# A second MLP with chunk 0 plain and chunks 1 and 2 by Strassen's seven products

## Chip, core and metric

One core of one Trainium2 chip runs the program alone. The metric is device microseconds from the first to the last instruction and what lies around them, as the median of several executions. TensorE (PE) multiplies, VectorE (DVE) and ScalarE (ACT) do elementwise work, GpSimd (POOL) a little of it, and SyncE (SP) issues nearly all DMAs. Each engine takes its own list of instructions in order.

## What is computed

A two-layer backbone on 1152 tokens (1024 latent, 128 context) of width 1024: attention and an MLP, then a bidirectional state-space layer with a gated unit (glu) and a second MLP, then a final norm. The MLP, on the modulated norm h of x, is

```python
def _mlp(h, w1, w2):
    a = jax.nn.relu(h @ w1)
    return (a * a) @ w2
...
xx = xx + g2x * _mlp(_modulate(xx, norm2_g[i], sh2x, sc2x), mlp_w1[i], mlp_w2[i])
...
y_sample = _rmsnorm(xx, final_norm_g)
```

with w1 of 1024 x 4096, w2 of 4096 x 1024, all in float32.

## The kernel before

Tokens lie in three chunks of 384 columns (`NCH`, `CW`), channels in eight tiles of 128 partitions (`KT`); chunk 2 ends with the context tokens, which have another modulation, so its elementwise operations come in pieces of 256 and 128 (`pieces`). A float32 product is made of three matmuls of a faster type: each operand is split into a high part (a cast on ACT, L51) and a low part (source minus high on DVE, L52), and `mm3` (L45 to L47) issues high x high, high x low, low x high.

```python
        mm(out, lh, rh, start=first, stop=False)
        mm(out, lh, rl, start=False, stop=False)
        mm(out, ll, rh, start=False, stop=last)
```

`mlp(layer)` walks over 16 blocks of 256 hidden units. A block loads its w1 and w2 (each in two raw tiles of 512 KB, L658, from a pair of buffers `wr`, and split into one high and one low tile). For each chunk the first product makes two tiles of 128 hidden units from eight tiles of h (48 matmuls); relu, square and split follow (L683, L684, L51, L52). Then for each chunk the second product makes eight tiles of 128 channels from the two (48 matmuls), and `add_x` (L455) adds each, times its gate, to x. A block is 288 matmuls of 128x384. At the start of the second MLP the h of chunk 0 is there already (from `glu`); those of chunks 1 and 2 are made by `norm_apply` (L234, L237, L238), chunk 2's after its `norm_stats`. The last block runs the final norm's statistics, and `final(c)` writes chunks 0 and 1 with ACT and POOL (L1241, L1242) beside the next chunk's products, and chunk 2 at the end with DVE (L1244).

Engine lists are ordered by the framework's scheduler from priorities in program order and its own estimate of when operands are ready; tile pools with a fixed number of buffers per tag decide which instruction waits for which.

Of the kernel before, what the change touches and what calls it, by code (L numbers as in the profile page):

```python
# [20 lines left out]
KT = 8  # L21
NCH = 3
CW = 384
HD = 64
DFF = 4096
# [8 lines left out]
class Body:  # L34
# [600 lines left out]
    def mlp(self, layer, bg=None):  # L635
        nc, tc, a = self.nc, self.tc, self.a
        with ExitStack() as ctx:
            M = ctx.enter_context(tc.tile_pool(name=f"mlp{layer}", bufs=1, reuse_waits="tile"))
            self.M = M
            ps = ctx.enter_context(tc.tile_pool(name=f"mlpps{layer}", bufs=6, space=PSUM))  # L640
            h = []
            for c in range(NCH):
                if c not in self.mh:
                    self.mh[c] = self.h_big(M, f"mh{c}")
                    if c == 2:
                        for _ in self.norm_stats(c):
                            pass
                    for _ in self.norm_apply(c, layer, 1, self.mh[c]):
                        pass
                h.append(self.mh[c])  # L650
            nb = DFF // 256

            def load(name, pool, tag, src):
                w = [pool.tile([128, 2048], F32R, name=name, tag=tag, bufs=2) for _ in range(2)]
                for q in range(2):
                    sl = slice(1024 * q, 1024 * q + 1024)
                    raw = self.R.tile([128, 1024], F32, name="wr", tag="wr", bufs=2)
                    nc.sync.dma_start(raw, src[:, sl])  # L658
# [5 lines left out]
            out = iter(())  # L664
            def fill(where):
                with self.tc.high_priority(offset=-self.LOW):
                    for _ in range((self.F0, self.F1)[where]):
                        next(gen, None)

            for fb in range(nb):  # L670
                w2 = load("w2", M, "w2", a["w2"][layer, fb])
                acts = []
                for c in range(NCH):
                    at = self.two_tiles(self.R, "at")
                    acts.append(at)
                    for m in range(2):
# [12 lines left out]
                for c in range(NCH):  # L689
                    stats = self.norm_stats(c, 1) if fb == nb - 1 else iter(())  # L690
                    for m in range(KT):
                        pt = ps.tile([128, 512], F32, name="m2", tag="acc")
                        for k in range(2):
                            sl = slice(1024 * k + 128 * m, 1024 * k + 128 * m + 128)
                            self.mm3(pt[:, :CW], w2[0][:, sl], w2[1][:, sl], acts[c][:, k, 0, :],
                                     acts[c][:, k, 1, :], k == 0, k == 1)
                        self.add_x(c, m, pt, layer, 1)
                        next(stats, None)
                        if m % 2:
                            next(out, None)  # L700
                    fill(1)
                    for _ in stats:
                        pass
                    if fb == nb - 1 and layer == 1:
                        out = self.final(c)
            for _ in out:
                pass
            for _ in gen:
                pass


    def cmul(self, eng, o_r, o_i, ar, ai, br, bi, t, neg=False):
# [517 lines left out]
                pass  # L1230
        self.yctx.close()

    def final(self, c):
        nc = self.nc
        for k in range(0, KT, 2):
            o = self.R.tile([128, 2, CW], F32, name="fo", tag=("wo", "wq")[k // 2 % 2] if c < 2 else "ot",
                            bufs=2 if c < 2 else 4)
            for kt in (k, k + 1):
                x, g, z = self.x[c][:, kt, :], self.gn[:, 4, kt:kt + 1], o[:, kt - k, :]
                if c < 2 or k == 6:  # L1240
# [37 lines left out]
    def run(self):  # L1278
        self.consts()
        self.start()  # L1280
        if self.stop != "s5":
            self.attention()
        if self.stop != "s5":
            if self.stop == "attn":
                return self.dump_x()
            self.mlp(0, self.background)
            if self.stop == "mlp0":
                return self.dump_x()
        else:
# [12 lines left out]

def host_consts():
# [96 lines left out]
```

## Time and profile before

| | |
|---|---|
| median of 3 runs | 2802.63 us (2799.61 to 2807.88) |
| profiled execution | 2799.74 us |
| its span, first to last instruction | 2797.8 us |
| PE busy in the span | 2609.5 us (93%) |
| DVE, ACT, POOL busy | 1824.4 us (65%), 1096.1 us (39%), 366.6 us (13%) |
| granted TensorE clock, mean | 0.979 |
| DMA | 271.67 MB, 97 GB/s |

The second MLP runs from about 1956 us to the end, with its last matmul at 2778.3 us. A matmul's record lasts about twice the distance to the next one, since two overlap; the number of records in a stretch is a few per cent short, so distances are taken from the instructions that wait for matmuls. L numbers are lines of the kernel before.

### The profile page before, as it was taken

To read this page: it belongs to the slowest core of one execution; us is meant where nothing else is said; L and a number is where in the kernel's file an instruction comes from. 1 tells how busy PE (TensorE), PEld (TensorE's weight loads), DVE (VectorE), ACT (ScalarE), POOL (GpSimd) and SP (SyncE) were. 2 spreads that over 40 slices of the span, in tenths; PEclk is the share of its full clock that TensorE was granted. 3 is DMA by queue.
4 is the path that set the end of the run, shared out by engine and by line. 5 is a ranking of instruction groups with operands and counts; after the bars stand their busy time and mean duration, and the time that the engine had idled before them with its cause. 6 is when DMAs were issued, how large, how long until landed. Compare 5 with 4: busy or idle time off the path is not lost. (4 is left out here: it accounts for less than half of the span.)

```text
span 2797.8 us, 44016 instructions
## 1 busy us (share of the span) xinstructions
PE 2609.5 (93%) x16561; PEld 2462.1 (88%) x16561; DVE 1824.4 (65%) x4342; ACT 1096.1 (39%) x2295; POOL 366.6 (13%) x476
## 2 busy tenths in 40 slices
PE   6889999998899999999899687999999999999997
PEld 4767987886699989899899676999999999999997
DVE  4847777785576787887875799545645354454455
ACT  3545666662223323332333655434422222212224
POOL 1222222210022132121220400000000000000002
PEclk8999999999999999999999799999999999999998
DMA  7353222235532233132223586433110111111101
GB/s 264 109 169 105 84 79 74 81 116 189 180 103 75 70 95 90 55 105 71 88 83 91 174 251 180 141 121 113 46 46 31 46 46 46 34 43 46 46 31 68
DMA packets 128452, 271.67 MB, mean 97 GB/s; under 512 B 13296, under 2 KB 67952, under 8 KB 126832
## 3 DMA queue, kind: packets, MB, share of 16 engines
q1 hardware_dynamic: 128240, 268.86, 30.3%
q8 instruction: 131, 2.15, 0.3%
q14 instruction: 81, 0.66, 0.1%
HBM read 214.22 MB, written 39.81 MB: 91 GB/s over the span
## 5 line engine op out<-in xcount | busy, mean ns | idle before, releaser
L455 DVE SCALAR_TENSOR_TENSOR x<-m,mod,x 128x384 f32<-128x384 f32 (+2 forms) x1024 | 496.2, 512 | 149.2 <-PE m L47 145.3
L47 PE MATMUL m<-at,w 128*128 128x384 f32 x1536 | 523.4, 341 | 0.0
L45 PE MATMUL m<-at,w 128*128 128x384 f32 x1536 | 522.7, 340 | 0.8 <-DVE x L455 0.8
L46 PE MATMUL m<-at,w 128*128 128x384 f32 x1536 | 521.7, 340 | 0.0
L45 PE MATMUL m<-mh,w 128*128 128x384 f32 x1024 | 349.1, 342 | 1.9 <-ACT mh L237 1.9
L47 PE MATMUL m<-mh,w 128*128 128x384 f32 x1024 | 349.9, 342 | 0.0
L46 PE MATMUL m<-mh,w 128*128 128x384 f32 x1024 | 349.8, 342 | 0.0
L52 DVE TENSOR_TENSOR at<-r,at 128x384 fp32r<-128x384 f32 x192 | 111.6, 583 | 361.4 <-ACT at L51 361.2
L51 ACT CAST w<-wr 128x1024 fp32r<-128x1024 f32 x128 | 131.0, 1046 | 524.4 <-PE m L46 515.7
L47 PEld LDWEIGHTS m<-at,w 128*128 128x128 f32 x1536 | 289.1, 188 | 9.2 <-issue 8.9
L45 PEld LDWEIGHTS m<-at,w 128*128 128x128 f32 x1536 | 289.2, 188 | 3.8 <-issue 1.8
L46 PEld LDWEIGHTS m<-at,w 128*128 128x128 f32 x1536 | 289.1, 188 | 2.8 <-issue 2.5
L683 ACT ACTIVATE r<-m 128x384 f32<-128x384 f32 x192 | 93.8, 490 | 373.1 <-PE m L47 370.3
L45 PEld LDWEIGHTS m<-mh,w 128*128 128x128 f32 x1024 | 193.9, 190 | 7.4 <-issue 4.8
L52 DVE TENSOR_TENSOR w<-wr,w 128x1024 fp32r<-128x1024 f32 x128 | 156.6, 1243 | 64.9 <-ACT w L51 60.6
L47 PEld LDWEIGHTS m<-mh,w 128*128 128x128 f32 x1024 | 194.5, 190 | 3.6 <-issue 3.5
L46 PEld LDWEIGHTS m<-mh,w 128*128 128x128 f32 x1024 | 194.4, 190 | 1.6 <-issue 0.8
L45 PE MATMUL m<-h,w 128*128 128x384 f32 x512 | 174.4, 341 | 1.5 <-ACT w L51 0.7
L47 PE MATMUL m<-h,w 128*128 128x384 f32 x512 | 173.9, 340 | 1.2 <-DVE w L52 1.2
L46 PE MATMUL m<-h,w 128*128 128x384 f32 x512 | 174.5, 341 | 0.0
L1242 POOL TENSOR_TENSOR fo<-fo,rb 128x384 f32<-128x384 f32 x18 | 20.6, 1176 | 1034.7 <-ACT rb L224 1026.9
L389 POOL TENSOR_SCALAR pt<-pt,sst 128x512 f32<-128x512 f32 (+1 forms) x144 | 102.6, 724 | 298.4 <-DVE sst L387 153.8
(328 smaller groups left out, 5161.1 us busy)
## 6 DMA issues: line engine op xcount, KB each, us to landing
wr<-in_w_dram SPq DMA_DIRECT2D x128, 512.0 KB, 4.4
wm<-in_w_mod_dram SPq DMA_DIRECT2D x80, 512.0 KB, 4.6
wr<-in_glu_dram SPq DMA_DIRECT2D x48, 512.0 KB, 3.3
wr<-in_w_qo_dram SPq DMA_DIRECT2D x24, 512.0 KB, 3.3
wr<-in_w_qo_dram SPq DMA_DIRECT2D x48, 256.0 KB, 2.8
bt<-bt_d SPq DMA_DIRECT2D x16, 768.0 KB, 5.5
dt_d<-d SPq DMA_DIRECT2D x32, 294.0 KB, 2.1
D<-dt_d SPq DMA_DIRECT2D x16, 588.0 KB, 4.7
```

Of the source, the lines that this page charges most:

```text
L45: mm(out, lh, rh, start=first, stop=False)
L46: mm(out, lh, rl, start=False, stop=False)
L47: mm(out, ll, rh, start=False, stop=last)
L51: (ceng.copy if ceng is self.nc.scalar else ceng.tensor_copy)(h, src)
L52: seng.tensor_tensor(out=l, in0=src, in1=h, op=ALU.subtract)
L389: nc.gpsimd.tensor_scalar(p[:, e, :nk], p[:, e, :nk], rc[:, e:e + 1], 1.0, op0=ALU.mult, op1=ALU.mult)
L455: nc.vector.scalar_tensor_tensor(out=self.x[c][:, m, lo:hi], in0=ps[:, lo:hi], scalar=self.gate(layer, j, m, s), in1=self.x[c][:, m, lo:hi ...
L683: nc.scalar.activation(r, pt[:, :CW], AF.Relu)
L1242: nc.gpsimd.tensor_tensor(out=z, in0=z, in1=self.rb[c], op=ALU.mult)
```

## The change

`run` calls a new `mlp1` in place of `mlp(1)`; the first layer's `mlp` only loses the lines that served the second. `mlp1` has two passes over the 16 blocks.

The first pass does chunk 0 alone with plain products. PE's order is: first product of block fb+1, second product of block fb. The raw loads of the next block's w1 are issued ahead of those of this block's w2. In between, `h_seven` makes the sums of chunks 1 and 2 that the products need (subtractions on POOL, each split by ACT and DVE).

The second pass does chunks 1 and 2. Their first product is a 2 x 2 block product (two halves of the inner channels, two tiles of hidden units, two chunks), done by Strassen's scheme with seven products instead of eight: `w_seven` makes seven weight parts of 128x512 from the two raw tiles of w1 (four sums on DVE, L731; each part split by L725 and L726), and `seven` issues for each product 4 x 3 matmuls into one of three PSUM banks pa, pb, pc in the order 1, 5, 6, 3, 7, 2, 4. Between products `keep` copies a bank's running value out (L931) and `done` adds a bank to such a copy (L934), then relu, square and split. Parts 1, 5, 6 and 3 are made under the second products of the block before; 7, 2 and 4 in their own block. The second products stay plain, so w2 is loaded and split once more. `h_rest` makes the h of products 3 and 2, under the last second product of the first pass. Chunk 0's final norm and output (`final0`) run in blocks 1 and 2 of the second pass; the last chunk of the kernel is now 1.

```diff
+    def w_seven(self, fb, w, first=False):
...
+        r0, r1 = self.w_half(fb, 0), self.w_half(fb, 1)
+        a11, a21, a12, a22 = r0[:, 0], r0[:, 1], r1[:, 0], r1[:, 1]
...
+        def put(i, src, t):
+            nc.scalar.copy(t[:, 0], src)
+            nc.vector.tensor_tensor(out=t[:, 1], in0=src, in1=t[:, 0], op=ALU.subtract)
+            w[i] = t
...
+        def single():
+            put(7, sx(a11, a21, ALU.subtract), one(R, "wo", 2))
+            yield
+            put(2, a12, one(R, "wo", 2))
+            yield
+            put(4, a22, one(M, "wz", 1))
+            yield
...
+        put(1, a11, t1)
+        yield
+        s1 = sx(a21, a22, ALU.add)
+        put(5, s1, t5)
+        yield
+        s2 = sx(s1, a11, ALU.subtract)
+        t6, t3 = two("ws", "wq")
+        put(6, s2, t6)
+        yield
+        put(3, sx(a12, s2, ALU.subtract), t3)
...
+    def seven(self, w, B, pa, pb, pc, evict):
...
+        for i in (1, 5, 6, 3, 7, 2, 4):
+            p = pa if i in (1, 6, 7, 4) else pb if i in (5, 3) else pc
+            for j in range(4):
+                f = first[id(p)] and j == 0
+                for k, (x, y) in enumerate(((0, 0), (0, 1), (1, 0))):
+                    self.nc.tensor.matmul(p[:, :CW], w[i][:, x, j, :], B[i][j][y], start=f and k == 0,
+                                          stop=j == 3 and k == 2, skip_group_check=True)
+            first[id(p)] = False
+            evict(i)
...
+            for fb in range(nb):
+                if fb + 1 < nb:
+                    w1 = load("w1", self.R, "wq", a["w1"][1, fb + 1])
+                w2 = load("w2", M, "w2", a["w2"][1, fb])
+                if fb + 1 < nb:
+
+                    nxt = first(w1)
+                    next(gen, None)
+                    second(0, w2, acts)
+                    next(gen, None)
+                    acts = nxt
+                else:
...
+                    rest = self.h_rest(B)
+                    sums = self.w_seven(0, ws, True)
...
+                    second(0, w2, acts, step)
...
+                    if i == 1:
+                        keep(1, pa)
+                    elif i == 5:
+                        keep(5, pb)
+                    elif i == 6:
+                        keep(6, pa)
+                    elif i == 3:
+                        done((0, 2), 6, pb)
+                    elif i == 7:
+                        sa = self.last[0].ins
+                        va = done((1, 2), 5, pa).ins
+                        with tc.issue_after(sa), tc.issue_after(va):
+                            w2[:] = [M.tile([128, 2048], F32R, name="w2", tag="w2", bufs=2) for _ in range(2)]
...
+                    elif i == 2:
+                        done((0, 1), 1, pc)
+                    else:
+                        at[1, 1] = act(M.tile([128, CW], F32, name="z", tag="z", bufs=1), pa[:, :CW])
...
+    def final0(self):
...
+            z = self.M.tile([128, CW], F32, name="z", tag="z", bufs=1)
+            nc.scalar.activation(z, self.x[0][:, kt, :], AF.Copy, scale=self.gn[:, 4, kt:kt + 1])
+            nc.gpsimd.tensor_tensor(out=z, in0=z, in1=self.rb[0], op=ALU.mult)
+            nc.sync.dma_start(self.o["y"][0, :, kt], z)
...
-        self.mlp(1)
+        self.mlp1()
```

Three places of the engines' lists follow. A name's number tells one buffer from another.

First, ACT inside a block of the second MLP. Before, the first products' relu, square and cast repeat with nothing between them, and w1's next cast stands behind them:

```order
L683 ACTIVATE r_21022<-m1_20997 128x384
L684 ACTIVATE r_21022<-r_21022 128x384
L51 CAST at_20966<-r_21022 128x384
L683 ACTIVATE r_21053<-m1_21028 128x384
L684 ACTIVATE r_21053<-r_21053 128x384
L51 CAST at_21027<-r_21053 128x384
L51 CAST w1_21088<-wr_21090 128x1024
L683 ACTIVATE r_21083<-m1_21058 128x384
```
Now, a block of the second pass (m1 are the three banks, r the copies, w2 the block's second weight):

```order
L931 COPY r_24984<-m1_24964 128x384
L931 COPY r_25001<-m1_24965 128x384
L931 COPY r_25022<-m1_24964 128x384
L861 ACTIVATE r_25022<-r_25022 128x384
L862 ACTIVATE r_25022<-r_25022 128x384
L863 CAST at_25037<-r_25022 128x384
L51 CAST w2_25060<-wr_25018 128x1024
L861 ACTIVATE r_25001<-r_25001 128x384
L51 CAST w2_25060<-wr_25020 128x1024
L862 ACTIVATE r_25001<-r_25001 128x384
L861 ACTIVATE r_24984<-r_24984 128x384
L863 CAST at_25055<-r_25001 128x384
```
Three copies out of the banks come first, and the two casts of w2 stand between the steps of products 3, 7 and 2.

Second, PE at the start of the second MLP, at the end of the first block's first product on chunk 0 (h). Before, chunk 1's h follows with the same w1:

```order
L45 MATMUL m1_20130<-h_19343,w1_20079 128x384
L46 MATMUL m1_20130<-h_19343,w1_20079 128x384
L47 MATMUL m1_20130<-h_19343,w1_20080 128x384
L45 MATMUL m1_20161<-mh1_19947,w1_20079 128x384
L46 MATMUL m1_20161<-mh1_19947,w1_20079 128x384
L47 MATMUL m1_20161<-mh1_19947,w1_20080 128x384
```
Now the next block's w1 follows at once (numbers 20019 high, 20020 low):

```order
L45 MATMUL m1_19988<-h_19343,w1_19947 128x384
L46 MATMUL m1_19988<-h_19343,w1_19947 128x384
L47 MATMUL m1_19988<-h_19343,w1_19948 128x384
L45 MATMUL m1_20039<-h_19343,w1_20019 128x384
L46 MATMUL m1_20039<-h_19343,w1_20019 128x384
L45 MATMUL m1_20070<-h_19343,w1_20019 128x384
L46 MATMUL m1_20070<-h_19343,w1_20019 128x384
L47 MATMUL m1_20039<-h_19343,w1_20020 128x384
L45 MATMUL m1_20039<-h_19343,w1_20019 128x384
```
The four matmuls that need only the high part of the new w1 stand ahead of the first that needs its low part.

Third, DVE where the last h is made. Before, at the start of the second MLP, chunk 2's h is all that DVE has there:

```order
L234 SCALAR_TENSOR_TENSOR nt_20023<-x2_72,gs11_98,rb_19981 128x256
L234 SCALAR_TENSOR_TENSOR nt_20023<-x2_72,gs11_98,rb_19981 128x128
L234 SCALAR_TENSOR_TENSOR nt_20030<-x2_72,gs11_98,rb_19981 128x256
L238 SCALAR_TENSOR_TENSOR mh2_19980<-nt_20023,mod1_94,mh2_19980 128x256
L238 SCALAR_TENSOR_TENSOR mh2_19980<-nt_20023,mod1_94,mh2_19980 128x128
L234 SCALAR_TENSOR_TENSOR nt_20030<-x2_72,gs11_98,rb_19981 128x128
L238 SCALAR_TENSOR_TENSOR mh2_19980<-nt_20030,mod1_94,mh2_19980 128x256
L234 SCALAR_TENSOR_TENSOR nt_20037<-x2_72,gs11_98,rb_19981 128x256
```
Now, under the last second product of the first pass (sx the weight sums, ws the weight parts' lows, hr the rest of h, m2 the product's tiles):

```order
L731 TENSOR_TENSOR sx_22437<-wr_22417 128x512
L455 SCALAR_TENSOR_TENSOR x0_70<-m2_22467,mod1_94,x0_70 128x384
L836 SCALAR_TENSOR_TENSOR hr_22421<-nt_22478,mod1_94,hr_22421 128x128
L726 TENSOR_TENSOR ws_22439<-sx_22437,ws_22439 128x512
L455 SCALAR_TENSOR_TENSOR x0_70<-m2_22485,mod1_94,x0_70 128x384
L726 TENSOR_TENSOR ws_22457<-wr_22419,ws_22457 128x512
L726 TENSOR_TENSOR ws_22475<-wr_22419,ws_22475 128x512
L726 TENSOR_TENSOR ws_22493<-wr_22417,ws_22493 128x512
L832 SCALAR_TENSOR_TENSOR nt_22496<-x1_71,gs11_98,rb_19766 128x384
L455 SCALAR_TENSOR_TENSOR x0_70<-m2_22500,mod1_94,x0_70 128x384
L731 TENSOR_TENSOR sx_22508<-wr_22417,wr_22419 128x512
L836 SCALAR_TENSOR_TENSOR hr_22421<-nt_22496,mod1_94,hr_22421 128x384
```
Weight sums, lows, h and the adds into x alternate in one list.

## Rows read from the trace of the kernel before

**Rows 1.** The page's 40 slices: PE busy tenths, granted clock.

```profile
PE   6889999998899999999899687999999999999997
...
PEclk8999999999999999999999799999999999999998
```
**Rows 2.** Windows: us, busy PE, PEld, DVE, ACT, POOL, then PEclk, DMA share, GB/s.

```profile
2000.00:2100.00 100.00, 100.00 (x570) 100.00 (x569) 45.70 (x84) 25.93 (x44) 0.00 (x0) 1.00 0.13 43
1976.00:1980.00 4.00, 2.58 (x8) 2.38 (x9) 3.95 (x12) 2.66 (x8) 0.00 (x0) 0.72 0.00 0
1880.00:1900.00 20.00, 20.00 (x116) 20.00 (x116) 8.35 (x11) 5.81 (x7) 0.00 (x0) 1.00 0.37 119
```
**Rows 3.** Timeline of DVE in one block: start, length, instruction, idle before.

```profile
2350.16 0.62 DVE L455 SCALAR_TENSOR_TENSOR x<-m,mod,x 128x384 f32<-128x384 f32 x1 [0.44 <-PE m L47]
...
2358.61 0.62 DVE L455 SCALAR_TENSOR_TENSOR x<-m,mod,x 128x384 f32<-128x384 f32 x1 [0.44 <-PE m L47]
...
2360.72 0.74 DVE L455 SCALAR_TENSOR_TENSOR x<-m,mod,x 128x256 f32<-128x256 f32 x2 [0.44 <-PE m L47]
```
**Rows 4.** Timeline of PE at the start of the second MLP.

```profile
1974.99 0.51 PE L223 MATMUL nrb<-ident,nst 128*128 128x128 f32 x3 [0.57 <-DVE nst L220]
1977.42 0.79 PE L45 MATMUL m<-mh,w 128*128 128x384 f32 x2 [1.92 <-ACT mh L237]
...
1981.22 0.52 PE L45 MATMUL m<-mh,w 128*128 128x384 f32 x2
```
**Rows 5.** Groups by line and shape from 1970 us on: busy us, mean ns.

```profile
L47 PE MATMUL m<-at,w 128*128 128x384 f32 x768 | 259.9, 338 | 0.0
...
L52 DVE TENSOR_TENSOR w<-wr,w 128x1024 fp32r<-128x1024 f32 x60 | 71.9, 1221 | 43.6 <-ACT w L51 43.6
...
L51 ACT CAST w<-wr 128x1024 fp32r<-128x1024 f32 x60 | 61.3, 1045 | 360.6 <-PE m L46 360.6
L52 DVE TENSOR_TENSOR at<-r,at 128x384 fp32r<-128x384 f32 x96 | 53.3, 557 | 260.2 <-ACT at L51 260.2
L684 ACT ACTIVATE r<-r 128x384 f32<-128x384 f32 x96 | 50.2, 525 | 2.4
L51 ACT CAST at<-r 128x384 fp32r<-128x384 f32 x96 | 49.1, 514 | 2.8
L683 ACT ACTIVATE r<-m 128x384 f32<-128x384 f32 x96 | 46.9, 491 | 196.5 <-PE m L47 196.5
...
L1241 ACT ACTIVATE fo<-x,gn 128x384 f32<-128x384 f32 x18 | 10.6, 604 | 1.3 <-DMA out_y_dram<-fo 1.3
...
L238 DVE SCALAR_TENSOR_TENSOR mh<-nt,mod,mh 128x256 fp32r<-128x256 f32 x8 | 3.8, 481 | 0.0
...
L238 DVE SCALAR_TENSOR_TENSOR mh<-nt,mod,mh 128x128 fp32r<-128x128 f32 x8 | 2.8, 346 | 0.1
```
**Rows 6.** Timeline of ACT: a cast and the instruction behind it.

```profile
2342.60 1.05 ACT L51 CAST w<-wr 128x1024 fp32r<-128x1024 f32 x1 [2.46 <-PE m L46]
2343.55 0.48 ACT L683 ACTIVATE r<-m 128x384 f32<-128x384 f32 x1
```
**Rows 7.** DMA issues (KB, median us to landing): second MLP, glu, end.

```profile
wr<-in_w_dram SPq DMA_DIRECT2D x57, 512.0 KB, 4.4
...
wr<-in_glu_dram SPq DMA_DIRECT2D x42, 512.0 KB, 3.3
...
out_y_dram<-fo SPq DMA_DIRECT2D x12, 384.0 KB, 2.3
```
**Rows 8.** Timeline near the end: DVE's running sum twice, POOL's eight operations.

```profile
2755.14 0.55 DVE L205 TENSOR_TENSOR nacc<-nacc,nsq 128x384 f32<-128x384 f32 x1
...
2764.35 1.25 DVE L205 TENSOR_TENSOR nacc<-nacc,nsq 128x384 f32<-128x384 f32 x1
...
2763.19 9.05 POOL L1242 TENSOR_TENSOR fo<-fo,rb 128x384 f32<-128x384 f32 x8 [1026.87 <-ACT rb L224]
```

More of the change, by code (lines that the diff above doesn't have):

```diff
@@ L663, in mlp @@
             gen = bg() if bg is not None else iter(())
-            out = iter(())
             def fill(where):
@@ L698, in mlp @@
                         next(stats, None)
-                        if m % 2:
-                            next(out, None)
                     fill(1)
@@ L703, in mlp, with w_half, two, one @@
                         pass
-                    if fb == nb - 1 and layer == 1:
-                        out = self.final(c)
+            for _ in gen:
+                pass
+    def w_half(self, fb, q, raw=None):
+        raw = self.R.tile([128, 1024], F32, name="wr", tag="wr", bufs=2)
+        self.nc.sync.dma_start(raw, self.a["w1"][1, fb][:, 1024 * q:1024 * q + 1024])
+        return raw.rearrange("p (k m c) -> p m k c", m=2, c=128)
+    def w_seven(self, fb, w, first=False):
+        nc, M, R = self.nc, self.M, self.R
+        r0, r1 = self.w_half(fb, 0), self.w_half(fb, 1)
+        a11, a21, a12, a22 = r0[:, 0], r0[:, 1], r1[:, 0], r1[:, 1]
+        def two(name, tag):
+            t = R.tile([128, 2, 2, 4, 128], F32R, name=name, tag=tag, bufs=2)
+            return t[:, 0], t[:, 1]
+        def one(pool, tag, bufs):
+            return pool.tile([128, 2, 4, 128], F32R, name="ws", tag=tag, bufs=bufs)
+        def put(i, src, t):
+            nc.scalar.copy(t[:, 0], src)
+            nc.vector.tensor_tensor(out=t[:, 1], in0=src, in1=t[:, 0], op=ALU.subtract)
+            w[i] = t
+        def sx(x, y, op):
+            t = M.tile([128, 4, 128], F32, name="sx", tag="sx", bufs=2)
+            nc.vector.tensor_tensor(out=t, in0=x, in1=y, op=op)
+            return t
+        def single():
[6 more added lines that the diff above has]
+        yield
+        if first:
+            yield from single()
+        t1, t5 = two("ws", "wq")
+        put(1, a11, t1)
[6 more added lines that the diff above has]
+        put(6, s2, t6)
+        yield
+        put(3, sx(a12, s2, ALU.subtract), t3)
+        yield
+        if not first:
+            yield from single()
@@ new lines, in seven @@
+    def seven(self, w, B, pa, pb, pc, evict):
+        n = 0
+        first = {id(pa): True, id(pb): True, id(pc): True}
+        for i in (1, 5, 6, 3, 7, 2, 4):
[7 more added lines that the diff above has]
+            evict(i)
@@ new lines, in h_part @@
+    def h_part(self, c, kt, out):
+        nc = self.nc
+        t = self.tt("nt")
+        for lo, hi, s in self.pieces(c):
+            nc.vector.scalar_tensor_tensor(out=t[:, lo:hi], in0=self.x[c][:, kt, lo:hi],
+                                           scalar=self.gs[1][1][:, kt, s:s + 1],
+                                           in1=self.rb[c][:, lo:hi], op0=ALU.mult, op1=ALU.mult)
+            nc.scalar.activation(out[:, lo:hi], t[:, lo:hi], AF.Identity, bias=self.shift(1, 1, kt, s))
@@ new lines, in h_seven @@
+    def h_seven(self, B):
+        nc, M = self.nc, self.M
+        gp = nc.gpsimd
+        slots = []
+        for i in range(4):
+            t = self.two_tiles(self.R, "ot")
+            slots += [t[:, k] for k in range(2)]
+        slots += [M.tile([128, 2, CW], F32R, name=f"hs{i}") for i in range(12)]
+        for j in range(4):
+            for i in (1, 5, 6, 7, 4):
+                t = slots.pop(0)
+                B[i][j] = (t[:, 0, :], t[:, 1, :])
+        for j in range(4):
+            ab = M.tile([128, 2, CW], F32, name="ab", tag="wz", bufs=1)
+            a, b = ab[:, 0], ab[:, 1]
+            c, d = (M.tile([128, CW], F32, name="cd", tag="sx", bufs=2) for _ in range(2))
+            put = lambda i, src: self.split(B[i][j][0], B[i][j][1], src, nc.scalar, nc.vector)
+            self.h_part(1, j, a)
+            self.h_part(2, j, b)
+            yield
+            put(1, a)
+            gp.tensor_tensor(out=a, in0=b, in1=a, op=ALU.subtract)
+            put(5, a)
+            yield
+            self.h_part(2, j + 4, c)
+            self.h_part(1, j + 4, d)
+            yield
+            gp.tensor_tensor(out=b, in0=c, in1=b, op=ALU.subtract)
+            put(7, b)
+            yield
+            gp.tensor_tensor(out=c, in0=c, in1=a, op=ALU.subtract)
+            put(6, c)
+            gp.tensor_tensor(out=d, in0=d, in1=c, op=ALU.subtract)
+            put(4, d)
+            yield
@@ new lines, in h_rest @@
+    def h_rest(self, B):
+        nc = self.nc
+        t = self.H.tile([128, 8, 2, CW], F32R, name="hr", tag="h")
+        for n, (i, c) in enumerate(((3, 2), (2, 1))):
+            for j in range(4):
+                h, l = (t[:, 4 * n + j, k, :] for k in range(2))
+                B[i][j] = (h, l)
+                u = self.tt("nt")
+                for lo, hi, s in self.pieces(c):
+                    sh = self.shift(1, 1, j + 4, s)
+                    nc.vector.scalar_tensor_tensor(out=u[:, lo:hi], in0=self.x[c][:, j + 4, lo:hi],
+                                                   scalar=self.gs[1][1][:, j + 4, s:s + 1],
+                                                   in1=self.rb[c][:, lo:hi], op0=ALU.mult, op1=ALU.mult)
+                    nc.scalar.activation(h[:, lo:hi], u[:, lo:hi], AF.Identity, bias=sh)
+                    nc.vector.scalar_tensor_tensor(out=l[:, lo:hi], in0=u[:, lo:hi], scalar=sh,
+                                                   in1=h[:, lo:hi], op0=ALU.add, op1=ALU.subtract)
+                yield
@@ L706, in mlp @@
             for _ in out:
                 pass
-            for _ in gen:
-                pass
+    def final0(self):
+        nc = self.nc
+        for kt in range(KT):
+            z = self.M.tile([128, CW], F32, name="z", tag="z", bufs=1)
+            nc.scalar.activation(z, self.x[0][:, kt, :], AF.Copy, scale=self.gn[:, 4, kt:kt + 1])
+            nc.gpsimd.tensor_tensor(out=z, in0=z, in1=self.rb[0], op=ALU.mult)
+            nc.sync.dma_start(self.o["y"][0, :, kt], z)
+            yield
@@ L1231, in glu, with final @@
         self.yctx.close()
-    def final(self, c):
+    def final(self, c, last):
         nc = self.nc
         for k in range(0, KT, 2):
-            o = self.R.tile([128, 2, CW], F32, name="fo", tag=("wo", "wq")[k // 2 % 2] if c < 2 else "ot",
-                            bufs=2 if c < 2 else 4)
+            o = self.R.tile([128, 2, CW], F32, name="fo", tag="ot" if last else ("wo", "wq")[k // 2 % 2],
+                            bufs=4 if last else 2)
             for kt in (k, k + 1):
                 x, g, z = self.x[c][:, kt, :], self.gn[:, 4, kt:kt + 1], o[:, kt - k, :]
-                if c < 2 or k == 6:
+                if not last or k == 6:
                     nc.scalar.activation(z, x, AF.Copy, scale=g)
```

109 lines of the change are left out of this document (added).

## Prediction

> **What bounds the kernel now.** I read the slices first, then windows, then one queue in order of time. In the slices [rows 1] PE stands at 9 tenths or more from the 29th slice to the 39th, with its clock at 9: that is the second MLP. In windows of 100 us [rows 2] PE is busy 100.00 of 100 at a granted clock of 1.00 (the seven stretches from 2000 to 2700 read alike, the first is shown), while DVE does 46 and ACT 26. So nothing but TensorE's own list of matmuls sets the time there, and only its two ends are ragged. The pitch comes from DVE's list [rows 3]: each add into x closes six matmuls, and eight adds, from 2350.16 to 2358.61, make 48 matmuls in 8.45 us, 176 ns each. One matmul is shown 338 ns long [rows 5]: two overlap, so its result is seen about 0.2 us after its own slot ends. The stage holds 16 x 288 = 4608 matmuls, 811 us.
>
> The profiled execution took 2799.7 us, 2.9 us less than the median of the runs shown (2802.6). I make the sum against 2799.7 and add the 2.9 at the end.
>
> **Removed work.** For chunks 1 and 2 a block's first product was 96 matmuls and becomes 7 products of 12, 84. Sixteen blocks lose 192 matmuls of the same shape: 192 x 176 ns = **-33.8 us**. The second product and chunk 0 keep theirs. The split weights of w2 are now made twice, 32 more loads of 512 KB with as many casts and subtracts, and weight and activation sums are added. None of this is on PE; the question is where PE must wait for it. DVE's new share of a 31.7 us block (180 matmuls) is 7 lows and 4 sums of 512 columns, about 0.7 us each (between 0.56 for 384 and 1.22 for 1024 columns [rows 5]), 7.7 us; with 16 adds into x, w2's lows and seven smaller operations it is near 25 us, still under 31.7. ACT has less.
>
> **The start.** Before, PE waits 0.57 and 1.92 us for chunk 2's norm and h, and after the second wait twelve matmuls take 3.80 us, from 1977.42 to 1981.22, where 12 x 176 ns is 2.11; the granted clock of 1976 to 1980 is 0.72 [rows 2, 4], so part of it ran at 1.2 GHz. These 2.5 + 1.7 us go. In their place PE meets two first products in a row (the second order excerpt): w1 has one pair of split tiles, so the second w1 can only be cast after the last matmul on the first. From that end: 0.2 us until it is seen, 1.05 for the cast, 1.22 for the low [rows 5], 2.5 us in all, of which PE fills 0.7 with the four matmuls that need only the high half: 1.8 us. Net **-2.4 us**.
>
> **First pass (chunk 0).** A half block is 48 matmuls, 8.45 us, and needs two raw tiles of 512 KB. A raw tile's round is landing 4.4 [rows 7], cast 1.05, low 1.22 [rows 5], about 6.8 us with the hand-overs, so PE stays the bound with 1.6 us to spare. The glu stage asks the same, one 512 KB load per 24 matmuls, from the same two raw tiles: there a load lands in 3.3 us [rows 7] and PE is busy 20.00 of 20 [rows 2]. Eight halves also carry the sums of chunks 1 and 2. In four of them ACT's casts, and DVE's lows behind them, wait for up to three POOL subtractions in a row, 9.05 / 8 = 1.13 us each [rows 8]; the low of w1's second half then ends about 10.8 us into the half, and PE wants it at 8.45 + 2.5 = 10.9. I take 0.3 us for each of the eight, **+2.5 us** (0 to 10).
>
> Here a row and a page can be weighed. DVE's running sum with two SBUF inputs took 0.55 us alone and 1.25 us in the stretch where POOL worked [rows 8]. By that row three POOL operations cost DVE up to 2.1 us in such a half, most of it while it waits anyway. The Trainium skill (SBUF — State Buffer, Who interferes with whom) says that a DVE instruction with two SBUF inputs and a GpSimd instruction that reads SBUF shut each other out for a whole instruction; the trace agrees with a delay, though at 0.7 us of the 1.13 that a POOL operation lasts, and by the rule it would be 3.4 us in such a half.
>
> **From the first pass to the second.** The last w2 of chunk 0 finds its tiles taken until the product before ends, so PE waits 0.2 + 1.05, **1.3 us**, for the cast. Then DVE has to do, beside the eight adds of that product, the last 12 operations on the h of products 3 and 2 (four of 384 columns in each of two kinds, the rest pieces of 256 and 128, 6.6 us [rows 5]) and 11 weight operations (7.7 us), in the order of the third excerpt. The raw w1 is issued when w2's lows end, 2.5 and 3.7 us after the product before, and lands 4.4 us later. Counting DVE's queue from there with the pitch of rows back to back (about 0.1 us under the durations [rows 6]), the low of part 1 ends 1.7 us after PE wants it, and those of parts 5, 2's h and 6 cost PE another 1.7 us in pieces: **3.4 us**. The first w2 of the second pass is late by **0.5 us**. A broken-up stretch like this can cost the clock as at the start; I take the same **1.7 us** (0 to 3.5). Together **+6.9 us**.
>
> **Steady second pass.** From block 3 on ACT and DVE have the same order in each block (first excerpt). Times from the start of a block: product 3 ends at 8.43, is seen at 8.6; the add into z 0.56 (as the low of an activation), relu 0.49, square 0.53, cast 0.51 give 10.8 [rows 5]; w2's two casts stand between the steps of product 7 and start near 10.7 and 12.1. DVE's low of w2's second half ends near 14.6, product 7's low activation near 15.1. PE ends the seven products at 14.76 and wants that low at 15.46. The reserve is 0.3 us. w2's raw tiles come free by 2.7 us and land by 7.1, long before 10.7. The next block's parts 1, 5, 6 and 3 are made under 16.9 us of second products, w1 landing 4 us into them; parts 7, 2 and 4 are ready at 2.6, wanted at 8.4 or later. The seven products take banks in turn, and each read of a bank (0.49) has a product of 2.11 us to hide under. I take 0.1 us a block, **+1.5 us** (0 to 15).
>
> **Chunk 0's final.** Its eight tiles of 384 columns share one buffer z: ACT 0.6 [rows 5], POOL 1.13 [rows 8], out and landed 2.3 (the row's 384 KB; these are 192) [rows 7], near 4.4 us with hand-overs, while ACT's queue has five of them in a row in block 2. The fifth then holds ACT some 5 us into block 3, and the read of product 1's bank, which product 6 needs at 4.2, comes near 7.0: 2.8 us. One more in block 2 costs 0.5. **+3.3 us** (0 to 5).
>
> **Tail.** The last chunk is now 1, with one add of 0.62 instead of two that take 0.74 [rows 3]; DVE's backlog at the end shrinks by about **1 us**.
>
> Sum: -33.8 - 2.4 + 2.5 + 6.9 + 1.5 + 3.3 - 1.0 = -23.0, so 2776.7 for that execution and **2780 us** against the median, 0.8% faster. What a measurement of this kernel tells from no change is about 0.3%, 8.4 us: under 2794 counts as faster, over 2811 as slower.
>
> **Rivals.**
> - *Weight loads bind the first pass (the slower end).* With two raw tiles and single split pairs, landing above 6.1 us makes the half block longer than its matmuls. At 6.8 us the half is 9.2, and 31 halves x 0.75 = 23 us eat the whole gain; at 7.5 it is 9.9, 31 x 1.45 = 45 us: 2825. For it: the 4.4 us are from a stretch that moved 43 GB/s [rows 2], and the first pass needs 2.1 MB in 16.9 us, 124 GB/s. Against it: glu at that rate lands in 3.3 [rows 7]. Chance 0.08.
> - *The block's edge waits.* If relu, square, cast and low come 1.3 us later than counted, PE loses 1 us in each of 15 blocks: 2794. The queues are in order, and 0.3 us is little. 0.13.
> - *POOL shuts DVE out whole.* If DVE stands for all of a POOL operation, three in a row take 3.4 us in four halves and one takes 1.1 in four others, 18 us where the sum has 2.5: 2796 at most. The row shows a good half of such a wait. 0.05. The Trainium skill (SBUF — State Buffer, Who interferes with whom) states this case.
> - *Strassen's products do not run at 176 ns.* Two or three products share a bank that ACT or DVE reads in between; if PE waited 0.3 us at each of 112 products, 34 us, the change would do nothing: 2813 at the worst, 2803 with part of it. The bank order speaks against it. 0.06.
> - *No crossing cost.* DVE keeps up, the clock stays, and the 3.3 us of chunk 0's final are hidden: 2780 - 6.9 - 3.3 = 2770. 0.11.
>
> **How the numbers follow.** The forecast keeps 0.57. Faster: the forecast, no crossing cost and half of the edge case, 0.75; same: the other half of that, POOL, half of the products, 0.15; slower: the loads and the rest, 0.10. The range goes from 2770 (no crossing cost) to 2800, which takes in the edge and POOL cases; it leaves out the loads and the products, 0.14, and a little below 2770.
>
> **What would show it.** Right: 192 matmuls fewer; second-pass blocks 31.7 us apart with PE at 1.00; first-pass blocks 16.9; PE idle of 1 to 3 us at the start, at the crossing (released by DVE's weight lows) and in block 3 (released by ACT's copies). Wrong: first-pass blocks over 17.5 us with casts waiting for wr; an idle piece in every second-pass block ahead of m2, released by at or w2; a pitch above 176 ns inside the seven products; or a clock under 1.00 in many blocks.

## The result and the profile after

The changed kernel takes **2768.07 us** (median of four runs, 2762.96 to 2772.71) against 2803.80 for the kernel before (four runs): 35.7 us less, ratio 0.9878, 95% interval 0.9865 to 0.9892. The direction was forecast and most of the mechanism is there, but the gain is half as large again as the 23.0 us of the sum, and the time lies 2 us under the range. The profiled executions differ by 36.8 us (2799.74 and 2762.96), so they can be compared term by term.

From here on an L number is a line of the kernel whose trace is shown; L45 to L52 are the same in all. The page of the changed kernel: span, instructions and busy time of the engines, two lines of the slices, and the load of weights from the DMA issues (KB each, median us to landing).

```profile
span 2761.2 us, 43936 instructions
...
PE 2567.9 (93%) x16369; PEld 2420.2 (88%) x16369; DVE 1984.6 (72%) x4618; ACT 1221.6 (44%) x2519; POOL 388.1 (14%) x492
...
PE   6889999998899989999999777899999999999997
...
PEclk9999999999999999999999899999999999999998
...
wr<-in_w_dram SPq DMA_DIRECT2D x192, 512.0 KB, 3.8
```

PE has 16,369 matmuls where it had 16,561: 192 fewer. The slices look as in [rows 1]. Windows of the second MLP (us, busy PE, PEld, DVE, ACT, POOL, then granted clock, DMA share, GB/s): the start, the first pass, the crossing, the second pass.

```profile
1956.00:1960.00 4.00, 4.00 (x17) 3.90 (x16) 0.48 (x3) 0.48 (x1) 0.00 (x0) 0.59 0.01 4
2000.00:2100.00 100.00, 100.00 (x579) 99.73 (x578) 70.50 (x110) 51.89 (x86) 10.32 (x8) 1.00 0.35 122
2220.00:2242.00 22.00, 18.76 (x101) 17.05 (x100) 20.99 (x38) 11.00 (x19) 0.00 (x0) 1.00 0.25 81
2400.00:2500.00 100.00, 100.00 (x576) 100.00 (x575) 67.74 (x133) 40.84 (x76) 0.00 (x0) 1.00 0.20 68
```

The last line is the surprise. PE is busy 100 of 100 at a clock of 1.00 as in [rows 2], yet it holds 576 matmuls where it held 570. The same is seen between blocks: ACT's first copy of a block (product 1's bank), in three blocks that follow each other.

```profile
2429.53 0.48 ACT L931 COPY r<-m 128x384 f32<-128x384 f32 x1 [0.46 <-PE m L769]
...
2460.90 0.48 ACT L931 COPY r<-m 128x384 f32<-128x384 f32 x1 [0.75 <-PE m L769]
...
2492.26 0.48 ACT L931 COPY r<-m 128x384 f32<-128x384 f32 x1 [0.75 <-PE m L769]
```

A block of 180 matmuls takes 31.36 us, 174.2 ns each, not 31.7. The groups from 1970 us on (busy, mean ns of one) split it: the second products' matmuls last 335 ns where they lasted 338 [rows 5], while those on h last 339.

```profile
L47 PE MATMUL m<-at,w 128*128 128x384 f32 x768 | 256.3, 335 | 0.0
...
L47 PE MATMUL m<-h,w 128*128 128x384 f32 x237 | 80.1, 339 | 0.0
```

What PE waited for from 1955 us to the end (us in total, times, longest): the first two lines are the last chunk's norm, behind the last matmul of the MLP.

```profile
PE nps L211 <- DVE nacc L205: 3.0, 1, 3.0
PE nrb L223 <- DVE nst L220: 2.2, 1, 2.2
PE m L45 <- ACT w L51: 1.9, 2, 1.0
PE m L769 <- DVE ws L726: 1.2, 1, 1.2
PE m L769 <- ACT r L931: 1.1, 1, 1.1
...
PE m L769 <- DVE hr L836: 0.6, 1, 0.6
```

**The account.** I took the starts of all MLP matmuls of the second MLP from the two traces; every one of the 4608 and 4416 has a record. Distances from one start to the next under 200 ns are the pitch: mean 176.00 ns before, 174.43 after. Longer ones are waits, norm matmuls in between, or the lower clock; their excess over 174 ns is summed by place.

| term | predicted | traces |
|---|---|---|
| 192 matmuls of 176.0 ns | -33.8 | -33.8 |
| pitch of the other 4416 (1.57 ns less each) | 0 | -6.9 |
| start | -2.4 | -1.3 |
| first pass | +2.5 | +0.4 |
| crossing to the second pass | +6.9 | +5.1 |
| steady second pass | +1.5 | 0 |
| blocks 2 and 3, chunk 0's final | +3.3 | +2.6 |
| norms in the last blocks | 0 | -1.6 |
| behind the last matmul | -1.0 | -0.8 |
| ahead of the second MLP | 0 | -0.4 |
| sum | -23.0 | -36.7 |

The two spans differ by 36.6 us; the rest is rounding. Half of what was missing is one line: the pitch. The other half is waits, most of them priced higher than they came. The pitch is no wait and no clock, so the first question for the runs was where it comes from.

### The profile page after: what moved, and what is told of

It reads as the page before. It is cut to its first block, busy times and chain, and to the rows that moved or that the text cites. A ratio compares the mean times of both kernels' runs of the same rounds, so it can differ in the third digit from the quotient of the medians.

```text
span 2761.2 us, 43936 instructions
## 1 busy us (share of the span) xinstructions
PE 2567.9 (93%) x16369; PEld 2420.2 (88%) x16369; DVE 1984.6 (72%) x4618; ACT 1221.6 (44%) x2519; POOL 388.1 (14%) x492
## 5 line engine op out<-in xcount | busy, mean ns | idle before, releaser
L45 PE MATMUL m<-at,w 128*128 128x384 f32 x1536 | 519.5, 338 | 2.6 <-DVE x L455 1.1
L45 PEld LDWEIGHTS m<-at,w 128*128 128x128 f32 x1536 | 288.5, 188 | 6.4 <-ACT w L51 1.9
L51 ACT CAST w<-wr 128x1024 fp32r<-128x1024 f32 x160 | 165.8, 1046 | 254.6 <-PE m L46 188.7
L52 DVE TENSOR_TENSOR w<-wr,w 128x1024 fp32r<-128x1024 f32 x160 | 198.9, 1251 | 69.9 <-ACT w L51 63.4
L45 PE MATMUL m<-mh,w 128*128 128x384 f32 x512 | 177.9, 347 | 0.0
L47 PE MATMUL m<-mh,w 128*128 128x384 f32 x512 | 177.6, 347 | 0.0
L46 PE MATMUL m<-mh,w 128*128 128x384 f32 x512 | 177.4, 346 | 0.0
L45 PE MATMUL m<-h,w 128*128 128x384 f32 x512 | 174.9, 342 | 2.2 <-ACT w L51 1.5
L52 DVE TENSOR_TENSOR at<-r,at 128x384 fp32r<-128x384 f32 x96 | 58.6, 612 | 101.7 <-ACT at L51 101.4
L682 ACT ACTIVATE r<-m 128x384 f32<-128x384 f32 x96 | 47.0, 491 | 177.2 <-PE m L47 177.0
L377 ACT ACTIVATE pt<-sps,sst 128x512 f32<-128x512 f32 (+1 forms) x144 | 89.3, 626 | 70.2 <-DVE sst L366 69.8
L769 PE MATMUL m<-hs,ws 128*128 128x384 f32 x576 | 114.4, 338 | 0.0
L365 DVE TENSOR_REDUCE sst<-sps 128x1 f32<-128x512 f32 (+1 forms) x144 | 87.1, 612 | 36.4 <-PE sps L363 33.6
L934 DVE TENSOR_TENSOR r<-r,m 128x384 f32<-128x384 f32 x48 | 26.5, 551 | 108.9 <-PE m L769 108.9
```

The costliest lines, as they stand in the source:

```text
L51: (ceng.copy if ceng is self.nc.scalar else ceng.tensor_copy)(h, src)
L52: seng.tensor_tensor(out=l, in0=src, in1=h, op=ALU.subtract)
L365: nc.vector.tensor_reduce(out=mx[:, e:e + 1], in_=ps[:, :nk], axis=AX.X, op=ALU.max)
L377: nc.scalar.activation(p[:, e, :nk], sps[e][:, :nk], AF.Exp, scale=SCALE, bias=ng[:, e:e + 1], accum_out=sm[:, e:e + 1])
L769: self.nc.tensor.matmul(p[:, :CW], w[i][:, x, j, :], B[i][j][y], start=f and k == 0, stop=j == 3 and k == 2, skip_group_check=True)
L934: add = nc.vector.tensor_tensor(out=z[i], in0=z[i], in1=p[:, :CW], op=ALU.add)
```

## The experiments

Theory A: the pitch hangs on where the streamed tile and the weight tile lie in a partition. By the programs' addresses, w1's tiles in the kernel before start at a multiple of 512 bytes (the first at 67,584) and h's 128 bytes past one (127,616); the activations' tiles (at) at a multiple and w2's 128 past. In the changed kernel at moved into the pool of w2: both are 128 past. In these two kernels every group of matmuls with a distance of 128 or 384 modulo 512 has a mean pitch of about 176, and those with 0 of about 173.5. Rival B: the pitch follows from what else runs. The table has all runs; the stage is from the first to the last matmul of the second MLP in the profiled execution.

| kernel | us (runs) | ratio to before, 95% | stage, us |
|---|---|---|---|
| before | 2803.8 (4) | | 822.7 |
| changed | 2768.1 (4) | 0.9878 (0.9865 to 0.9892) | 787.2 |
| e1_before_moved | 2785.7 (4) | 0.9936 (0.9920 to 0.9953) | 812.8 |
| e2_after_moved | 2752.7 (4) | 0.9812 (0.9797 to 0.9827) | 786.3 |
| e3_eighth | 2795.7 (8) | 0.9967 (0.9957 to 0.9978) | 819.5 |
| e4_at_shift | 2770.4 (4) | 0.9881 (0.9863 to 0.9898) | 792.7 |
| e5_dist | 2758.7 (1) | | 787.5 |
| e6_z2 | 2763.1 (4) | 0.9857 (0.9840 to 0.9873) | 785.9 |
| e7_w2first | 2894.9 (1) | | 922.3 |
| e9_dve_subs | 2765.6 (4) | 0.9863 (0.9848 to 0.9878) | 785.8 |
| e10_parts_order | 2771.4 (4) | 0.9880 (0.9864 to 0.9897) | 789.4 |
| e11_all | 2750.7 (4) | 0.9829 (0.9803 to 0.9855) | 778.6 |
| e12_swap | 2768.1 (1) | | 789.4 |

Ratios, and differences of medians below, go against the runs of the kernel before that were taken with each kernel: 2804.7 (e1 to e4), 2802.4 (e5, e6, e9, e10) and 2802.0 (e7, e11, e12). What lies ahead of the stage differs by up to 9 us between the traces of kernels that are the same there (the stage begins at 1952.3 in e7, at 1961.5 in e10), so small effects are read from the stage.

**e1: the tile moved, nothing else.**

```diff
-        st = self.N.tile([128, 4, 3], F32, name="nst", tag="nst", bufs=2)
+        st = self.cp.tile([128, 4, 3], F32, name="nst", tag="nst", bufs=2)
```

> The kernel before with one small tile (the norm's 128 bytes per partition) allocated in another pool, so that the streamed tiles of the MLPs and their weight tiles start at the same place modulo 512 bytes (before: 128 bytes apart). No instruction and no order changes. Theory A (addresses): the mean distance of two matmul starts falls from 176.0 to 173.4 ns in both MLPs; 2 x 4608 matmuls x 2.6 ns = 24 us, so about 2780 us, 0.991 of before. Rival B (the pitch in the changed kernel is shorter because of what else runs: order, smaller tiles, less DVE or POOL traffic): the pitch stays 176.0 and the time within 0.3% of before.

Measured: w1's and at's tiles now start 128 bytes past a multiple of 512, as h's and w2's do. The pitch is 173.5 ns in the first MLP and 173.36 in the second; the time falls by 19 us. The same window of e1 as the first of [rows 2]: DVE and ACT are as busy as there, and 579 matmuls stand where 570 did.

```profile
2000.00:2100.00 100.00, 100.00 (x579) 100.00 (x578) 46.69 (x85) 25.99 (x44) 0.00 (x0) 1.00 0.13 43
```

All engines' instructions stand in the same order as before, so rival B is out. Of the 24 us that were forecast, the traces show 7.7 in the first MLP and 9.9 in the second (the stage); waits and matmuls 320 ns apart, the 1.2 GHz level, took back 2.2 of the second's.

**e2: the same edit in the changed kernel.**

> The changed kernel with the same tile moved. Theory A: in the first layer's MLP 4608 x 2.6 = 12 us, in the second the 1536 first products of chunk 0 and some 900 of the seven products' matmuls that still stood 128 bytes apart, 2400 x 2.6 = 6 us: about 2750 us, 0.981 of before. Rival B: 2768 us, 0.988 of before, pitch of the first layer still 176.

Measured: 2752.7, close to the 2750. The first MLP is at 173.5 as forecast and 10.1 us shorter than before. In the second the pitch falls to 173.48, worth 4.2 us, but the stage only loses 1.0: in the first pass PE now loses 5.0 us (excess of distances) where the changed kernel's trace had 0.4. The view of waits, 2015 to 2212 us, has half of that, since it counts only time in which no matmul is shown running:

```profile
PE m L47 <- DVE w L52: 2.5, 4, 0.8
```

The four are waits for the low of w1, the place that the prediction priced. e9 takes it up.

**e3: an eighth product.**

```diff
-        for i in (1, 5, 6, 3, 7, 2, 4):
+        for n, i in enumerate((1, 5, 6, 3, 7, 2, 4, 4)):
...
-            evict(i)
+            if n != 6:
+                evict(i)
```

> The changed kernel with the last of the seven products computed twice (its output is not the reference's): 16 x 12 = 192 matmuls are back, and all else of the change stays. Theory: the gain is the count, less small waits, plus the addresses. Then 192 x 0.174 to 0.176 = 33.4 to 33.8 us more than the changed kernel, about 2802 us; what is left against before, 2804, is the waits of the change (about +6) and the shorter pitch (about -7), so within 0.3% of before. Rival (the order of the passes itself gains, the count matters less because PE waits at block edges): clearly under 2795.

Measured: the stage is 819.5, 32.2 us over the changed kernel's and 3.2 under before's; the median is 9 us under before's, more than the theory allows by some 6. In the stage the count is worth 32.2 of the 33.5 that 192 x 174.4 ns make; the waits in blocks 2 and 3 went from 2.6 to 0.3 (a longer block gives ACT more time, which is argued, not tested), and the first pass had 3.3 instead of 0.4. So the count carries the gain in the stage. The 6 us are not explained, but the traces don't hold them: the profiled executions differ by 2.3 (2799.74 and 2797.41), and the one of the kernel before lies 5 us under its own median.

**e4: only the activations moved away again.**

```diff
             w1 = load("w1", self.R, "wq", a["w1"][1, 0])
+            M.tile([128, 32], F32, name="pa", tag="pa", bufs=1)
+            M.tile([128, 2, CW], F32R, name="at", tag="at", bufs=4)
+            M.tile([128, 96], F32, name="pb", tag="pb", bufs=1)
```

> The changed kernel with its four activation tiles of the second MLP moved by 128 bytes per partition (a pad of 128 bytes ahead of them, 384 behind), so that they stand 128 bytes from w2's tiles modulo 512, as in the kernel before up to the sign. Theory A: the second products' 2304 matmuls go from 173.4 to 176.0 ns, 6 us: about 2774 us, and their blocks from 31.36 to 31.6 us. Rival B: pitch 173.4 and 2768 us as in the changed kernel.

Measured: pitch of the second products 175.98 instead of 173.41, the stage 5.5 us longer (6 forecast), the median 2770.4 where 2774 was forecast, which the intervals can't tell from the changed kernel; the stage and the pitch decide. ACT's first copies of two blocks in a row, 31.62 us apart where they were 31.36:

```profile
2433.59 0.48 ACT L934 COPY r<-m 128x384 f32<-128x384 f32 x1 [0.76 <-PE m L769]
...
2465.21 0.48 ACT L934 COPY r<-m 128x384 f32<-128x384 f32 x1 [0.76 <-PE m L769]
```

With e1 this settles nearly all of the 6.9 us: they come from the place of at, which the change altered in passing (2285 distances, 2.6 ns less each, are 5.9; the rest are matmuls of the seven products that also stand at 0).

**e5: other distances.**

```diff
+            self.np = self.N.tile([128, 16], F32, name="np", tag="np", bufs=1)
...
+            M.tile([128, 16], F32, name="mp", tag="mp", bufs=1)
```

> The changed kernel with a pad of 64 bytes in the norm's pool and another of 64 in the first MLP's pool, which makes the start of the streamed tile differ from the weight tile's, modulo 512 bytes, by 192 (h), 256 (mh1 and mh2) and 256 (activations) in the first MLP, by 192 and 0 in the second. It tells what distance costs: if only equal places modulo 512 are fast, all but the 0 group stand at 176; if places are equal modulo 256, the 256 groups stand at 173.4 and the 192 group at 176; if modulo 64, all at 173.4.

Measured: none of the three rules. In the first MLP the groups at 192 and 256 stand at 173.7, 173.6 and 173.5. In the second the same tiles h and w1, still 192 apart, stand at 176.3, the sums at 172.8 (192) and 176.1 (0), the activations at 173.6 (0). So the distance of a matmul's own two tiles isn't the whole rule. Nor are the tiles of its neighbours: h and w1 lie at the same addresses in both MLPs, and their matmuls come in runs of 48. In one such run of the first MLP (from 878.59 us) the distances are 173, 173, 174 until other matmuls come in between, and behind them 178, 174, 173, 178, 171. What went before thus counts too. In all other kernels 0 gave 173.3 to 173.8 and 128 or 384 gave 175.8 to 177.4. What decides at other distances stays open.

**e6: two buffers for z.**

```diff
-            z = self.M.tile([128, CW], F32, name="z", tag="z", bufs=1)
+            z = self.M.tile([128, CW], F32, name="z", tag="z", bufs=2)
```

> The changed kernel with two buffers instead of one for the tile z of chunk 0's final (and of the last seven-product activation). Theory (ACT stands in its queue for z to be free, and PE for ACT's copies): the 2.6 us of PE's waits in blocks 2 and 3 of the second pass fall to 0.5 or less, time 2766. Rival (the work of the final itself fills ACT and POOL): they stay at 2.6. The times alone will hardly tell, 2 us being 0.07%; the trace does.

Measured: by distances 2.6 us of waits in blocks 2 and 3 fall to about 1.1, not to the 0.5 that was forecast. What PE waited for from 2255 to 2345 us in e6:

```profile
PE m L45 <- DVE x L455: 0.3, 1, 0.3
```

In the changed kernel's timeline of PE the same stretch has three waits:

```profile
2315.07 0.44 PE L45 MATMUL m<-at,w 128*128 128x384 f32 x1 [0.50 <-ACT at L863]
2315.71 0.44 PE L46 MATMUL m<-at,w 128*128 128x384 f32 x1 [0.21 <-DVE at L864]
2337.22 1.31 PE L769 MATMUL m<-ot,ws 128*128 128x384 f32 x6 [1.08 <-ACT r L931]
```

The waits on ACT (block 2's activation, block 3's copy of product 1) are gone; a wait for an add into x, 0.3, is new. One trace would not carry this, since the wait for the copy is missing in e9 and e12 as well, which keep one z. The wait for the activation decides: it stands in all eight traces that have one z and the changed kernel's blocks, and in neither of the two with two z (e6, e11). So the single z held ACT's queue there, as the theory has it.

**e9: the sums of h on DVE.**

```diff
-        gp = nc.gpsimd
+        gp = nc.vector
```

> The changed kernel with the sums of h made by DVE instead of POOL (20 subtractions of 384 columns). Theory (in the first pass PE waits at times for the low of w1's second half, which is late because ACT and DVE stand for POOL's subtractions in their queues and because a low beside a POOL operation takes 1.7 instead of 1.2 us): those waits, which were 0.4, 3.2, 2.0 and 4.8 us in the four traces of kernels with this pass, fall to 0.5 or less. Rival (the loads or DVE's own load are the cause): they stay or grow. Time 2766 to 2770 by either.

Measured: no distance of 200 ns or more in the first pass, behind the norm of chunk 2. The eight traces with POOL's subtractions and the changed order of loads show an excess of 0.4, 5.0, 3.3, 2.1, 1.2, 2.9, 2.4 and 4.2 us there (changed kernel, e2 to e6, e10, e12), mean 2.7; the two without them, e9 and e11, none. So the subtractions on POOL are the cause. How they delay the low is seen in part in e2's timelines, first DVE, then POOL:

```profile
2057.10 0.56 DVE L52 TENSOR_TENSOR ot<-ab,ot 128x384 fp32r<-128x384 f32 x1
...
2058.11 1.73 DVE L52 TENSOR_TENSOR w<-wr,w 128x1024 fp32r<-128x1024 f32 x1
...
2061.81 1.21 DVE L52 TENSOR_TENSOR w<-wr,w 128x1024 fp32r<-128x1024 f32 x1
```

```profile
2057.74 1.02 POOL L806 TENSOR_TENSOR ab<-ab 128x384 f32<-128x384 f32 x1 [28.48 <-DVE ot L52]
```

The first low overlaps 0.65 us of POOL's operation and takes 0.52 longer than the second. How much of PE's waits is this and how much ACT's standing for POOL in its queue, the runs do not separate. The Trainium skill (SBUF — State Buffer, Who interferes with whom) says that a DVE instruction with two SBUF inputs and a GpSimd instruction that reads SBUF contend for a shared port pair, which is an exclusive lock; this row nearly agrees (0.52 of 0.65), closer than [rows 8] did.

**e10 and e12: the order at the crossing.** e10 makes the first block's parts in the order of use, e12 the h of product 2 ahead of product 3's.

```diff
-                    sums = self.w_seven(0, ws, True)
+                    sums = self.w_seven(0, ws)
```

> The changed kernel with the first block's weight parts made in the order 1, 5, 6, 3, 7, 2, 4 instead of 7, 2, 4, 1, 5, 6, 3. Theory (at the crossing PE waits for DVE's queue, in which four operations of 0.7 us stand ahead of part 1's low that are wanted only 8 us later): PE's waits after the last second product of chunk 0 fall from 3.5 us to about 1, those around w2 (1.2 and 0.4) stay; time 2765.5. Rival (DVE's whole list is the limit, whatever its order): products 7, 2 and 4 wait instead, and the 3.5 us stay.

```diff
-        for n, (i, c) in enumerate(((3, 2), (2, 1))):
+        for n, (i, c) in enumerate(((2, 1), (3, 2))):
```

> The changed kernel with the last h of product 2 made ahead of that of product 3. In PE's list the first block of the second pass has nine of product 2's matmuls ahead of product 6's. Theory: of the 3.5 us that PE waits there the 0.9 on h go, since what PE meets first is then made first: about 2.5 us. Rival: product 3's h, now last, is late by as much, and the 3.5 us stay or grow.

Measured: both theories fell. From product 1 of the first block to its first second products PE's excess was 3.9 us in the changed kernel (the 3.5 of the forecasts and 0.4 behind them), 6.1 in e10 (some 1.4 of it matmuls up to 320 ns apart, behind a wait of 1.6; the granted clock was 0.51 from 2248 to 2250), 3.7 in e12. PE's waits around the crossing in e12, 2220 to 2265 us (the changed kernel's stand in the section on the result):

```profile
PE m L45 <- ACT w L51: 1.0, 1, 1.0
PE m L769 <- DVE ws L726: 0.7, 1, 0.7
PE m L769 <- DVE r L934: 0.6, 1, 0.6
PE m L769 <- ACT r L931: 0.6, 1, 0.6
PE m L769 <- ACT ws L725: 0.4, 1, 0.4
```

The waits on h went, and nearly as much came back on the adds and copies behind. In e10 part 1 was ready in time, but PE's list for this block has nine of product 2's matmuls ahead of product 6 (the scheduler put them there), and part 2 was now made late. That the sum over DVE's queue costs here, whatever its order, is what the rivals say and fits both runs; it isn't shown by itself. An order that gains was not found.

**e7: the second weights loaded first.**

```diff
-                if fb + 1 < nb:
-                    w1 = load("w1", self.R, "wq", a["w1"][1, fb + 1])
                 w2 = load("w2", M, "w2", a["w2"][1, fb])
                 if fb + 1 < nb:
+                    w1 = load("w1", self.R, "wq", a["w1"][1, fb + 1])
```

> The changed kernel with one part of the change undone: in the first pass w2 is loaded ahead of the next block's w1. Theory (the order of the loads carries the first pass): w2's pair of tiles is free only when the second product of the block before ends, so its raws hold both raw tiles and its casts hold ACT's queue until then; only afterwards does the next w1 load (3.6 to 4.4 us), get cast (1.05) and its low made (1.2). PE then stands 6.5 to 8 us in each of 15 blocks, 100 to 120 us, and more if the clock falls: 2865 us or more, above before. Rival (loads are far enough ahead for any order): within 10 us of the changed kernel.

Measured: 2894.9 (one run), 93 us above the kernel before. PE's waits in its first pass, and then a window of it:

```profile
PE m L45 <- ACT w L51: 95.4, 15, 7.6
```

```profile
2000.00:2100.00 100.00, 73.58 (x367) 70.85 (x366) 47.68 (x72) 31.79 (x50) 4.25 (x4) 0.83 0.25 84
```

Fifteen waits of 6.4 us in the mean, just under the 6.5 to 8 worked out, are 95 of the 135 us by which the stage grew. Of the other 40 about 25 are the clock (0.83 in this window): matmuls 320 ns apart, the 1.2 GHz level, follow the waits. The order of the loads, not their number, carries the first pass.

**e11: moved tile, two z, sums on DVE.**

> Three of the edits together: the norm's tile moved (addresses), two buffers for z, the sums of h on DVE. If the parts add: the second MLP's stage, 787.2 us in the changed kernel's trace, loses 4.2 us of pitch, 2 us of waits in blocks 2 and 3 and the first pass's waits, which had grown to 4.8 us where the pitch was shorter: 780 to 781 us. The first layer and the rest as with the moved tile alone. Median 2747, 0.979 to 0.980 of before.

Measured: the stage is 778.6, under the 780 to 781, with no wait in the first pass. The median of 2750.7 was forecast at 2747 and can't be told from e2's 2752.7; both beat the changed kernel.

## Why the prediction was wrong, and where it was right

**The step that failed** is in the removed work: "Sixteen blocks lose 192 matmuls of the same shape: 192 x 176 ns" was right, "the second product and chunk 0 keep theirs" was right as a count, and with it went an unspoken term, that the other 4416 keep 176 ns. They did not: 2304 second products stand at 173.4 because at left the pool where it lay 128 bytes off w2. 4416 x 1.57 ns = 6.9 us. The new place of at is part of the change and was priced at nothing without a row behind it; [rows 3] give the pitch of one placement, and the rival on products let the pitch grow but not shrink. e1 and e4 show the cause. With the 6.9 us in the sum the forecast would have been 2773, inside the range.

**Right.** The count (e3: 32.2 of 33.5 us in the stage). Two of the crossing's prices: 1.3 us for the last w2 of chunk 0 and 3.4 for the sums forecast, 1.2 and 3.5 in the trace. The 1.7 for the clock was not lost, the granted clock being 1.00 from 2220 to 2242. The block's edge: w2's second low was put 14.6 us into a block and product 7's low activation at 15.1; in the block that starts at 2458.6 they end at 14.7 and 15.2:

```profile
2472.09 1.22 DVE L52 TENSOR_TENSOR w<-wr,w 128x1024 fp32r<-128x1024 f32 x1
2473.22 0.55 DVE L864 TENSOR_TENSOR at<-r,at 128x384 fp32r<-128x384 f32 x1
```

So the reserve of 0.3 us held in every block from block 3 on, and the 1.5 taken for it was not needed. The first pass: 2.5 us forecast, from the cause named (e9); 0.4 in the profiled execution, 2.7 in the mean of eight traces. With 0.4 to 5.0 among them, that this mean is so near is in part luck. Chunk 0's final: 2.6 for 3.3, and the cause named (e6).

**Mis-sized.** The first w2 of the second pass: 0.5 us forecast, under 0.1 in the trace. The 0.4 that stands near it is another wait, which the prediction left out: product 4 needs the bank that DVE's add of product 7 still reads (DVE from 2244.5 to 2247.6, PE from 2246.6 to 2247.5):

```profile
2246.52 0.56 DVE L934 TENSOR_TENSOR r<-r,m 128x384 f32<-128x384 f32 x1 [1.48 <-PE m L769]
```

```profile
2246.32 0.69 PE L769 MATMUL m<-hr,ws 128*128 128x384 f32 x3
2247.13 0.62 PE L769 MATMUL m<-ot,ws 128*128 128x384 f32 x2
```

The start: 1.1 us less gained than forecast, since the clock fell there too: 0.59 from 1956 to 1960, matmuls 320 ns apart, behind a wait of 0.7 us for the stage ahead and chunk 0's norm matmuls; seven of the ten other traces with the same start lack it (0.4 instead of 2.0 us). The norms in the last blocks: before, the norms of chunks 0 and 1 held up 5.1 us of matmuls, now those of chunks 0 and 2 hold up 3.4; the prediction left them out.

**The rivals.** Weight loads: a tile lands in 3.6 us in the first pass (median, 1960 to 2220 us), not 6.1, and no wait is a load's; e7 shows what it is worth when the order is wrong. Edge waits: none. POOL: in the one row shown the delay is near the whole of the overlap (0.52 of 0.65), but the first pass loses 2.7 us in the mean and not 18. Products: PE is at 100.00 in each window from 2400 to 2700. No crossing cost: it is there, 5.1 us; the time fell below that case by way of the pitch.

## What to carry to other kernels

A busy PE at full clock can still be 1.5% off: compare the count of matmuls in equal windows, or the mean distance of starts, and if it is above the best stretch of the same shape, try moving one tile by 128 bytes; here that gave 0.6% of the whole time in each of two kernels (e1, e2). When a change gives a tile another pool, its place is part of the change. Where DVE's whole queue was late, two other orders of it did not mend the stretch (e10, e12).

## What the runs showed of the hardware that was not expected

- The mean distance of back-to-back matmuls of 128x384 with their own weight load was 173.3 to 173.8 ns with the streamed and the weight tile starting at the same place modulo 512 bytes, and 175.8 to 177.4 with 128 bytes between, in all kernels but e5; in the sequence of starts the first reads 173, 173, 174 over and over, the second 181, 176, 173, 175, 175. The Trainium skill (SBUF — State Buffer, Who interferes with whom) gives PE one read port for the streamed operand and one for the weights, independent of each other; the runs show that their places matter together, if not through what.
- In e5 one and the same pair of tiles, at the same addresses, stood at 173.7 ns in one MLP and 176.3 in the other.
